# The first norm's gain spread by TensorE, the first product group ordered by hand, and a rewritten order of the attention stage

## The chip, the cores and the metric

The kernel runs on one core of a Trainium2 chip. The metric is device time in microseconds (us) of one execution; the median of three runs is given where runs are told of. A core has TensorE (PE in the profile; its weight loads are PEld), VectorE (DVE), ScalarE (ACT), GpSimd (POOL) and SyncE (SP, which here only issues DMAs).

## The reference

Two layers act on 256 tokens of width 1024, all in f32. A SwiGLU block (inner width 2816) stands at both ends of each layer. Between them layer 0 has a pooling mixer and layer 1 an attention mixer with 8 heads in each of 3 groups of different dilation. Every part has an RMS norm in front and one behind it, before the residual sum:

```python
def rms_norm(x, gain):
    y = x32 * lax.rsqrt(jnp.mean(x32 * x32, axis=-1, keepdims=True) + RMS_EPS) * gain

f = swiglu(rms_norm(h, g[0]), ffn_w_gate[layer, 0], ffn_w_up[layer, 0], ffn_w_down[layer, 0])
h = h + 0.5 * rms_norm(f, g[1])
```

In the attention each query row takes a softmax over the keys of all three groups together (the mix over groups by their sums comes to that), multiplies the values by it, and goes through an output projection.

## The kernel before, in words

Tokens stand in two row blocks of 128 (`h[0]`, `h[1]`). To keep f32 accuracy with single-pass matmuls, each operand is split into a high part (a cast to fp32r on ScalarE, L100) and a low part (the rest, on VectorE, L101), and three products are summed. A weight block of 128 x 2048 comes by DMA into one of three `raw` buffers; its two halves are split into "units", which lie in six `hl` and two `xy` buffers. An operand `aT` is the normalised row block, transposed by TensorE in eight 128-column pieces and split the same way.

Opening. x is loaded in halves, the first norm's gain is loaded by a DMA that writes the same row to 128 partitions (`load_gain`, L176), 64 small matmuls run on zeros (`WARM`, L82), and the factor of each row (a sum of squares on ScalarE, the power -0.5 on GpSimd) and the gain are multiplied into the rows on VectorE (`norm`, L267). Then follow the transposes (L216) and the first product group of the first SwiGLU block: 96 matmuls of 512 columns into four PSUM banks (`acc_b0`). Instructions inside `tc.manual_schedule` keep the order in which they are written, for the engines that it names; all others are placed by a planner.

Norms between blocks (`Bound`). `first` multiplies a block's output by its gain and factor, adds it to h, and writes the rows for the next block into a second buffer, with the row factor of the previous norm; `second` transposes; `third` finds the new factor, which later steps multiply in. All inverse roots are powers on GpSimd.

Attention. For each of four head pairs `pr` and both row blocks `i`: a query projection in two halves (`q_proj`, 24 matmuls of 384 columns), the rope (L700 to L704, VectorE), transposes of the queries (`q_turn`, L819) with copies by ScalarE (L821), scores (`scores`, tile sc), then masking and a running maximum on VectorE (L759), the factor nm from it (L761), the exponential on ScalarE (L763), a reciprocal on VectorE (L769) and the multiplication by it on GpSimd (`over_sums`, L770), transposes of the probabilities (`p_turn`, L783) with copies by ScalarE (L786), and the product with the values (`values`, tile ob). A loop over `pr` writes them in this order (conditions and loads left out):

```python
q_proj(pr, 0, 0, cur); over_sums(pr - 1, 0); q_turn(pr - 1, 1); p_turn(pr - 2, 1)
q_proj(pr, 0, 1, cur); scores(pr - 1, 1); values(pr - 2, 1); p_turn(pr - 1, 0)
q_proj(pr, 1, 0, cur); over_sums(pr - 1, 1); q_turn(pr, 0); values(pr - 1, 0)
q_proj(pr, 1, 1, cur); scores(pr, 0)
```

Behind the loop the last pair's steps are mixed with the output projection (`o_proj`, tile acc_o), with only TensorE's order by hand. Below, a half pair is the time from one score group to the next.

Of the kernel before, what the change touches and what calls it, by code (L numbers as in the profile page):

```python
# [11 lines left out]
F32 = mybir.dt.float32  # L12
# [18 lines left out]
WARM = 64  # L31
# [17 lines left out]
def trunk_kernel(ctx: ExitStack, tc: tile.TileContext, x, pos, gains, pscale, ws, wq, invf, amask, pmat, icnt, out):  # L49
# [31 lines left out]
    for _ in range(WARM):  # L81
        nc.tensor.matmul(warm[:, 0:P], zeros, zeros, start=True, stop=True)  # L82
# [39 lines left out]
    def load_q_units(pr, b):  # L122
        raw = rawp.tile([P, 2, 1024], F32, tag="raw", name=f"rawq{pr}{b}")
        nc.sync.dma_start(raw[:, :, :768], wq[pr * 2 + b])
        return [parts(raw, k, 768, pr % 2 == 0 and b == 0) for k in range(2)]
# [68 lines left out]
    def post(i, f, gain, half, name, done=None):  # L194
# [81 lines left out]
    def ffn(n, aT, sums, boundary, middle=None, late=None, q=None):  # L276
# [121 lines left out]
        units = first_units + (load_units(4) if first_units else load_units(8, True))  # L398
        first_units[:] = []
        gu = [acc_pair(f"b{n}{i}") for i in range(2)]  # L400
        if n == 0:
            for z in range(2):
                both([gu[0][z], gu[1][z]], units[z * 4 : z * 4 + 4])
# [63 lines left out]
    class Bound:  # L467
# [15 lines left out]
        def first(self, i, f):  # L483
            self.y = []

            def scaled(i, c):
                if not self.y:
                    self.y.append(sc4.tile([P, D], F32, tag="y", name=f"n_{self.n}{i}"))
                nc.vector.scalar_tensor_tensor(
                    self.y[0][:, c], h[i][:, c], self.old[:, i : i + 1], self.gpre[:, c], op0=ALU.mult, op1=ALU.mult  # L490
                )

            post(i, f, self.gpost, self.half, self.n, scaled)

        def second(self, i):
            transposed(i, self.y[0], self.aT, self.n, self.sums)
# [20 lines left out]
    gpre = load_gain(0, "pre")  # L517
    aT = new_aT("x")
    sums = Sums("x")
    with tc.manual_schedule(engines={mybir.EngineType.DVE, mybir.EngineType.Activation}):  # L520
        y = norm(0, gpre, "x", rstd_of(h_halves(0), "qx0", rx[:, 0:1]))
        raws = [load_raw(at=0)]
        first_units += [parts(raws[0], 0, xy=True)]
        nc.sync.dma_start(h[1], x[P:, :])
        transposed(0, y, aT, "x", sums)
        rstd_of(h_halves(1), "qx1", rx[:, 1:2])
        load_raw(at=1, raw=raws[0])
        first_units += [parts(raws[0], 1, xy=True)]
        y = norm(1, gpre, "x", rx[:, 1:2])
        raws.append(load_raw())  # L530
        first_units += [parts(raws[1], 0)]
        transposed(1, y, aT, "x", sums)
        first_units += [parts(raws[1], 1)]
    for i in range(2):
        sums.add(i)
# [202 lines left out]
    qT = [qx[g // 2][:, g % 2].rearrange("p (r s) -> p r s", r=4) for g in range(3)]  # L738
    am = qx[2][:, 0].bitcast(BF16).rearrange("p (i k) -> p i k", i=2)
    pTt = [t.rearrange("p (c t) -> p c t", c=4) for t in (qx[1][:, 1, 0:512], qx[1][:, 1, 512:1024], qx[2][:, 1])]  # L740
    nc.gpsimd.dma_start(am, amask.rearrange("i p k -> p i k"))
    npt = [0]
    probs = {}

    def scores(pr, i, pool=accp, tag="acc"):
# [3 lines left out]
        sc = [pool.tile([P, 512], F32, tag=tag, name=f"sc{i}_{pr}{e}") for e in range(2)]  # L749
        for o, g, keys in ((0, 0, slice(0, S)), (256, 1, t), (384, 2, t)):  # L750
            for e in range(2):
                a = slice(e * 64, e * 64 + 64)
                n = keys.stop - keys.start
                mm(sc[e][:, o : o + n], q[g][a, t], kT[g][a, pr, keys], True, True)
        probs[i, pr] = []
        for e in range(2):
            p = sc2.tile([P, 512], F32, tag="w2", name=f"p{i}_{pr}{e}")
            mx = st.tile([P, 1], F32, tag="mx", name=f"mx{i}_{pr}{e}")
            nc.vector.tensor_tensor_reduce(p, sc[e], am[:, i], 1.0, -3.0e38, op0=ALU.add, op1=ALU.max, accum_out=mx)  # L759
            nm = st.tile([P, 1], F32, tag="nm", name=f"nm{i}_{pr}{e}")  # L760
            nc.vector.tensor_scalar_mul(nm, mx, -0.125)  # L761
            den = st.tile([P, 1], F32, tag="den", name=f"den{i}_{pr}{e}")
            nc.scalar.activation(p, p, AF.Exp, bias=nm, scale=0.125, accum_out=den)  # L763
            probs[i, pr].append((p, den))

    def over_sums(pr, i):
        for e, (p, den) in enumerate(probs[i, pr]):
            rd = st.tile([P, 1], F32, tag="rd", name=f"rd{i}_{pr}{e}")
            nc.vector.reciprocal(rd, den)  # L769
            nc.gpsimd.tensor_scalar_mul(p, p, rd)  # L770
            probs[i, pr][e] = p

    oT = [None, None]

    pT = {}

    def p_turn(pr, i):

        pT[i, pr] = []
        for e in range(2):  # L780
            tp = tpp.tile([P, 4, P], F32, tag="tp", name=f"ptp{i}_{pr}{e}")
            for c in range(4):
                nc.tensor.transpose(tp[:, c], probs[i, pr][e][:, c * P : (c + 1) * P], ident)  # L783
            pT[i, pr].append(pTt[npt[0] % len(pTt)])
            npt[0] += 1
            nc.scalar.copy(pT[i, pr][e], tp)  # L786

    def values(pr, i):
# [4 lines left out]
        for c, (g, j) in enumerate(((0, 0), (0, 1), (1, i), (2, i))):  # L793
            for e in range(2):
                n = slice((2 * pr + e) * 64, (2 * pr + e) * 64 + 64)
                mm(ob[e * 64 : e * 64 + 64, 0:P], vt[g][:, j, n], pT[i, pr][e][:, c], c == 0, c == 3)
# [3 lines left out]
    acc_f = [None, None]  # L800

    def o_proj(i, chunks):
# [5 lines left out]
    def q_proj(pr, i, half, units):  # L808
# [4 lines left out]
        if half == 1:  # L813
# [197 lines left out]
```

## Time and profile before

| | before |
|---|---|
| median of 3 runs | 970.23 us (968.0 to 972.78) |
| profiled execution | 972.42 us |
| its span, first to last instruction | 970.7 us |
| TensorE busy | 946.7 us, 4560 matmuls |
| VectorE busy | 682.6 us |
| ScalarE busy | 536.3 us |
| GpSimd busy | 62.7 us |
| mean granted TensorE clock | 0.986 |

Busy time counts overlapping work of one engine once. The granted clock is 1 at the upper of TensorE's two levels (2.4 GHz) and 0.5 at the lower (1.2 GHz). A wait is time in which an engine stood idle until something released it.

### The profile page before, as it was taken

What the parts mean: (1) busy time and instruction counts of PE and PEld (TensorE: products, weight loads), DVE (VectorE), ACT (ScalarE), POOL (GpSimd) and SP (SyncE); (2) the same over time, 40 slices, a digit from 0 to 9 for tenths busy, and PEclk for the clock granted to TensorE, in tenths of its full rate; (3) what the DMA queues carried; (4) which work ended last, traced back from release to release, by engine and by line L of the source; (5) the groups of instructions that cost most, each with busy time, mean ns of one, the idle gap of its engine ahead of it and who ended that gap; (6) DMA issues with size and microseconds to landing.
All of it is one profiled execution on the core that took longest, in us unless ns stands there. A gap on an engine that the chain in (4) does not pass through costs nothing.

```text
span 970.7 us, 12064 instructions
## 1 busy us (share of the span) xinstructions
PE 946.7 (98%) x4560; PEld 784.5 (81%) x4560; DVE 682.6 (70%) x768; ACT 536.3 (55%) x672; POOL 62.7 (6%) x74
## 2 busy tenths in 40 slices
PE   7999999999999999999999999999988899999997
PEld 5888788888888888888888888888976688888886
DVE  5879874488878886458887964875465587888642
ACT  5665753366657565355756643644345576675531
POOL 0000000010100000000000000200033310000000
PEclk8999999999999999999999999999999799999999
DMA  7887775565568597536687865564334236968721
GB/s 248 294 254 223 242 278 182 209 211 179 194 211 261 186 298 260 188 131 244 156 300 225 295 218 181 186 208 144 128 102 148 87 119 186 335 141 296 245 87 44
DMA packets 55898, 197.16 MB, mean 203 GB/s; under 512 B 7392, under 2 KB 7392, under 8 KB 53792
## 3 DMA queue, kind: packets, MB, share of 16 engines
q1 hardware_dynamic: 53456, 179.35, 52.5%
q0 software_dynamic: 2384, 17.04, 9.3%
q8 instruction: 36, 0.59, 0.2%
q14 instruction: 22, 0.18, 0.1%
HBM read 178.54 MB, written 1.05 MB: 185 GB/s over the span
## 4 chain that ended last, share of the span: by engine, by line
PE 92%; DVE 3%; ACT 2%; issue 1%; DMA 1%; POOL 0%; SPq 0%; DVEq 0%; POOLq 0%; ACTq 0%
PE acc_d L130 24%; PE st L323 15%; PE g L130 13%; PE u L130 9%; PE acc_b L130 9%; PE kp L130 3%; PE vp L130 3%; PE qp L130 3%; PE acc_w L130 2%; PE acc_u L130 2%; PE htp L304 2%; PE ob L130 1%; DVE hl L101 1%; DMA raw<-in_ws 1%; PE acc_o L130 1%
## 5 line engine op out<-in xcount | busy, mean ns | idle before, releaser
L101 DVE TENSOR_TENSOR hl<-raw,hl 128x1024 fp32r<-128x1024 f32 x182 | 221.0, 1221 | 110.8 <-ACT hl L100 110.1
L100 ACT CAST hl<-raw 128x1024 fp32r<-128x1024 f32 x182 | 189.5, 1051 | 147.2 <-PE acc_d L130 99.0
L130 PE MATMUL acc_d<-hl,h 128*128 128x512 f32 x1056 | 243.2, 390 | 0.0
L130 PEld LDWEIGHTS acc_d<-hl,h 128*128 128x128 f32 x1056 | 197.3, 188 | 40.4
L108 DVE TENSOR_TENSOR hl_lo<-xy,hl_hi 128x2048 fp32r<-128x2048 f32 x40 | 91.6, 2290 | 48.3 <-ACT hl_hi L107 48.3
L108 DVE TENSOR_TENSOR hl_lo<-raw,hl_hi 128x2048 fp32r<-128x2048 f32 x48 | 109.7, 2285 | 13.9 <-ACT hl_hi L107 13.8
L107 ACT CAST hl_hi<-xy 128x2048 fp32r<-128x2048 f32 x40 | 76.5, 1912 | 57.1 <-PE u L130 28.2
L107 ACT CAST hl_hi<-raw 128x2048 fp32r<-128x2048 f32 x48 | 91.9, 1914 | 23.9 <-PE st L323 11.5
L130 PE MATMUL acc_b<-hl,aT_m 128*128 128x512 f32 x192 | 44.4, 390 | 0.0
L130 PE MATMUL g<-hl_hi,aT_m 128*128 128x512 f32 x128 | 41.9, 393 | 0.0
L130 PEld LDWEIGHTS acc_b<-hl,aT_m 128*128 128x128 f32 x192 | 35.9, 188 | 7.4
L323 PE MATMUL st<-hl_hi,S_m 128*128 128x512 f32 x128 | 41.9, 393 | 0.0
L306 ACT CAST h<-htp 128x512 fp32r<-128x512 f32 (+1 forms) x48 | 26.3, 549 | 28.1 <-PE htp L304 28.1
L130 PE MATMUL u<-hl_hi,aT_m 128*128 128x512 f32 x128 | 41.8, 393 | 0.0
L130 PE MATMUL qp<-hl,aT_f 128*128 128x384 f32 x192 | 39.3, 357 | 0.0
L130 PEld LDWEIGHTS qp<-hl,aT_f 128*128 128x128 f32 x192 | 35.2, 200 | 1.3 <-issue 0.8
L130 PE MATMUL kp<-hl,aT_hk 128*128 128x512 f32 x144 | 34.5, 394 | 0.0
L340 POOL DMA_DIRECT2D xy<-raw x16 | 14.0, 876 | 298.5 <-ACT h L306 85.3
L130 PE MATMUL vp<-hl,aT_hk 128*128 128x512 f32 x144 | 33.1, 390 | 0.0
L770 POOL TENSOR_SCALAR p<-p,rd 128x512 f32<-128x512 f32 x16 | 24.9, 1563 | 116.0 <-DVE rd L769 94.3
L307 DVE TENSOR_TENSOR h<-htp,h 128x512 fp32r<-128x512 f32 (+1 forms) x48 | 30.7, 640 | 2.2 <-ACT h L306 2.0
L130 PEld LDWEIGHTS vp<-hl,aT_hk 128*128 128x128 f32 x144 | 27.0, 188 | 5.6
(261 smaller groups left out, 1592.6 us busy)
## 6 DMA issues: line engine op xcount, KB each, us to landing
raw<-in_ws SPq DMA_DIRECT2D x278, 512.0 KB, 4.9
xy<-in_ws SPq DMA_DIRECT2D x32, 512.0 KB, 6.5
xy<-raw POOLq DMA_DIRECT2D x16, 1024.0 KB, 8.2
rawq<-in_wq SPq DMA_DIRECT2D x8, 768.0 KB, 4.7
gain_post<-in_gains SPq DMA_DIRECT2D x14, 256.0 KB, 7.0
gain_pre<-in_gains SPq DMA_DIRECT2D x12, 256.0 KB, 7.3
rawpm<-in_pmat SPq DMA_DIRECT2D x2, 512.0 KB, 4.4
out_dram<-h SPq DMA_DIRECT2D x4, 256.0 KB, 2.1
```

What stands on the lines that cost most here:

```text
L100: nc.scalar.copy(hl[:, 0, :n], raw[:, k, :n])
L101: last["dve"] = nc.vector.tensor_sub(hl[:, 1, :n], raw[:, k, :n], hl[:, 0, :n])
L107: nc.scalar.copy(hi, raw)
L108: last["dve"] = nc.vector.tensor_sub(lo, raw, hi)
L130: last["mm"] = nc.tensor.matmul(o, l, r, start=start, stop=stop)
L304: nc.tensor.transpose(tp[:, k], prod[c, i][:, k * P : (k + 1) * P], ident)
L306: nc.scalar.copy(d[:, 0], tp[:, :nt])
L307: nc.vector.tensor_sub(d[:, 1], tp[:, :nt], d[:, 0])
L323: nc.tensor.matmul(ps, a(z, k), u[v], start=start and k == 0 and n == 0, stop=k == 3 and n == 2, skip_group_check=not start,)
L340: nc.gpsimd.dma_start(dst, src, accum_op=ALU.add)
L770: nc.gpsimd.tensor_scalar_mul(p, p, rd)
```

## The change

Opening: the gain is loaded as one row, and two matmuls with a row of ones write it to all 128 partitions of two PSUM banks, from where VectorE reads it. 26 matmuls on zeros run first and three times four more (`FILL`) between the products. A new function `opening` writes the order of TensorE, VectorE, ScalarE and SP up to the end of the first product group; one of the sums of squares goes to VectorE. The first row block's products with the first units come before the second row block's norm.

```diff
-WARM = 64
+WARM = 26
+FILL = 4
+    keep_warm(WARM)
+    gfirst = gp.tile([P, D], F32, tag="pre", name="gain_first")
+    nc.sync.dma_start(gfirst[0:1], gains[0:1])
...
+        with tc.manual_schedule(
+            engines={
+                mybir.EngineType.PE,
+                mybir.EngineType.DVE,
+                mybir.EngineType.Activation,
+                mybir.EngineType.SP,
+            }
+        ):
+            raws.append(load_raw())
+            nc.sync.dma_start(h[1], x[P:, :])
+            raws.extend(load_raw() for _ in range(2))
+            for k in range(2):
+                mm(gb[k], ones[0:1, 0:P], gfirst[0:1, k * 512 : (k + 1) * 512], True, True)
+            rs = rstd_x(0)
+            y = rows(0, rs)
+            turn_x(0, 0, y)
+            parts_x(0, 0)
+            turn_x(0, 1, y)
+            unit(0)
+            parts_x(0, 1)
+            keep_warm(FILL)
+            products(0, 0)
+            unit(1)
+            keep_warm(FILL)
+            products(0, 1)
+            keep_warm(FILL)
+            rs = rstd_x(1)
+            unit(2)
+            y = rows(1, rs)
+            sums.add(0)
+            unit(3)
+            raws.append(load_raw())
+            products(0, 2)
+            turn_x(1, 0, y)
+            parts_x(1, 0)
+            turn_x(1, 1, y)
+            parts_x(1, 1)
+            products(0, 3)
+            unit(4)
+            for j in range(4):
+                products(1, j)
+            for j in range(5, 8):
+                unit(j)
+            for i in range(2):
+                for j in range(4, 8):
+                    products(i, j)
+        sums.add(1)
```

Here `rows` is the normalising, `turn_x` the transposes, `parts_x` the high and low parts of the transposed rows, `unit` the split of a half weight block, and `products(i, j)` six matmuls of row block i with unit j. `rstd_x` keeps the power on GpSimd, as it was.

Norms: the rows for the next block are written over the buffer of the block's own output.

```diff
             if done is not None:
-                done(i, c)
+                done(i, c, y)
+        return y
```

Attention: masking and the factor nm become one instruction, the multiplication by the reciprocal goes from GpSimd to VectorE, three query copies become two, and three buffers for transposed probabilities become two. The order of TensorE, VectorE and ScalarE is written out up to the last pair, and a function `between` holds what stands behind each projection:

```diff
+        nc.vector.tensor_tensor_reduce(
+            p, sc[pr, i][e], am[:, i], -0.125, 3.0e38, op0=ALU.add, op1=ALU.min, accum_out=nm
+        )
...
-            nc.gpsimd.tensor_scalar_mul(p, p, rd)
...
+        nc.vector.tensor_scalar_mul(p, p, rd)
...
+    def between(b, q, new, old):
...
+        z = high(b)
+        if b < 9:
+            next_raw(b + 1)
+        q_rope(*q)
+        if new is not None:
+            score_mm(*new)
+            for e in range(2):
+                masked(*new, e)
+        if old is not None:
+            p_turn(*old)
+        if new is not None:
+            exped(*new, 0)
+        if old is not None:
+            for e in range(2):
+                p_copy(*old, e)
+        if new is not None:
+            exped(*new, 1)
+        u = low(z)
+        if new is not None:
+            for e in range(2):
+                over_sum(*new, e)
+        return u
...
+            q_proj(pr, 0, 0, cur)
+            if pr > 0:
+                q_turn(pr - 1, 1)
+            if pr > 1:
+                value_mm(pr - 2, 1)
+            q_proj(pr, 0, 1, cur)
+            units += between(2 * pr + 2, (pr, 0), (pr - 1, 1) if pr > 0 else None, (pr - 1, 0) if pr > 0 else None)
+            q_proj(pr, 1, 0, cur)
+            q_turn(pr, 0)
+            if pr > 0:
+                value_mm(pr - 1, 0)
+            q_proj(pr, 1, 1, cur)
+            units += between(2 * pr + 3, (pr, 1), (pr, 0), (pr - 1, 1) if pr > 0 else None)
+        raw = load_raw()
+        first_units += [parts(raw, k, xy=True) for k in range(2)]
+        o_proj(0, 0, 1)
         q_turn(3, 1)
+        value_mm(2, 1)
+        raw = load_raw()
+        o_proj(0, 2)
+        score_mm(3, 1, gup, "gu")
+        masked(3, 1, 0)
+        masked(3, 1, 1)
         p_turn(3, 0)
+        exped(3, 1, 0)
+        p_copy(3, 0, 0)
+        p_copy(3, 0, 1)
+        exped(3, 1, 1)
+        over_sum(3, 1, 0)
+        over_sum(3, 1, 1)
+        first_units += [parts(raw, k) for k in range(2)]
+        o_proj(1, 0)
+        value_mm(3, 0)
+        o_proj(1, 1)
+        o_proj(0, 3)
         go.first(0, acc_f[0])
+        p_turn(3, 1)
+        p_copy(3, 1, 0)
+        p_copy(3, 1, 1)
+        o_proj(1, 2)
+        value_mm(3, 1)
+        o_proj(1, 3)
         go.second(0)
```

`high` and `low` are the casts and the low parts of one query weight block (from block 8 on, of the output projection's), `q_rope`, `score_mm`, `value_mm` and `p_copy` the parts of the functions told above. `first_units` are four units of the last SwiGLU block, which before were split behind the attention.

## Rows read from the trace of the kernel before

**Rows 1.** The page: busy time, share and count of each engine, and the chain of work that ended last, by engine.

```profile
PE 946.7 (98%) x4560; PEld 784.5 (81%) x4560; DVE 682.6 (70%) x768; ACT 536.3 (55%) x672; POOL 62.7 (6%) x74
...
PE 92%; DVE 3%; ACT 2%; issue 1%; DMA 1%; POOL 0%; SPq 0%; DVEq 0%; POOLq 0%; ACTq 0%
```
**Rows 2.** The view by stretches of time. Columns: from and to, length, then busy time and count on PE, PEld, DVE, ACT and POOL, the granted clock, the busy share of the DMA engines, GB/s.

```profile
60.00:660.00 600.00, 598.92 (x2780) 494.88 (x2778) 447.74 (x470) 338.93 (x394) 25.52 (x35) 1.00 0.68 222
703.56:756.09 52.53, 44.97 (x317) 39.58 (x316) 33.01 (x79) 29.02 (x65) 17.68 (x12) 0.90 0.33 116
756.09:783.71 27.62, 24.39 (x157) 19.32 (x156) 16.75 (x39) 15.66 (x34) 8.94 (x7) 0.88 0.27 87
```
**Rows 3.** The chain of waits in order of time, from 0 to 45 us: start, length, engine or transfer, tile, line, count.

```profile
2.59 8.40 DMA raw<-in_ws
...
19.61 19.56 PE acc_b L130 x85
39.17 2.72 PE g L130 x12
```
**Rows 4.** The timeline from 0 to 25 us: start, length, engine, line, operation, tiles, and in brackets the idle time before it and its releaser.

```profile
4.66 0.63 ACT L183 ACTIVATE jk_qx<-h 128x512 bf16<-128x512 f32 x1 [0.51 <-DMA h<-in_x]
...
7.03 0.75 DVE L267 SCALAR_TENSOR_TENSOR n_x<-h,r_x,gain_pre 128x512 f32<-128x512 f32 x1 [1.47 <-DMA gain_pre<-in_gains]
...
9.81 0.75 DVE L267 SCALAR_TENSOR_TENSOR n_x<-h,r_x,gain_pre 128x512 f32<-128x512 f32 x1 [2.02 <-DMA gain_pre<-in_gains]
```
**Rows 5.** Groups of instructions from 0 to 40 us, shapes kept apart: line, engine, operation, count, then busy us, mean ns of one, and the idle time before them.

```profile
L101 DVE TENSOR_TENSOR hl<-raw,hl 128x1024 fp32r<-128x1024 f32 x8 | 9.7, 1220 | 2.6 <-ACT hl L100 2.6
L100 ACT CAST hl<-raw 128x1024 fp32r<-128x1024 f32 x8 | 8.1, 1049 | 5.6 <-DMA raw<-in_ws 5.6
L82 PE MATMUL warm<-zeros 128*128 128x128 bf16 x64 | 5.6, 273 | 1.0 <-DVE zeros L79 1.0
```
**Rows 6.** Stretches of the opening, columns as in rows 2.

```profile
5.04:8.45 3.41, 2.16 (x32) 1.79 (x29) 0.91 (x2) 0.34 (x2) 0.55 (x1) 1.00 0.95 255
8.45:11.87 3.42, 0.70 (x5) 0.42 (x4) 0.75 (x1) 0.86 (x1) 0.00 (x0) 0.98 1.01 388
11.87:15.28 3.41, 2.69 (x5) 1.70 (x6) 2.51 (x4) 3.38 (x9) 0.55 (x1) 0.50 1.02 416
15.28:18.70 3.42, 3.24 (x11) 2.03 (x10) 3.33 (x4) 1.97 (x4) 0.00 (x0) 0.52 0.52 172
```
**Rows 7.** Who waited for whom, TensorE from 689 to 784 us: us in total, times, longest.

```profile
PE ob L130 <- ACT qT L786: 5.8, 3, 2.6
PE ptp L783 <- POOL p L770: 2.7, 3, 1.4
PE qtp L819 <- DVE ra_q L704: 1.2, 1, 1.2
```
**Rows 8.** Groups of instructions from 689 to 790 us, as in rows 5.

```profile
L770 POOL TENSOR_SCALAR p<-p,rd 128x512 f32<-128x512 f32 x16 | 24.9, 1563 | 116.0 <-DVE rd L769 94.3 <-ACT qT L786 14.6 <-PE qtp L819 7.1
...
L763 ACT ACTIVATE p<-p,nm 128x512 f32<-128x512 f32 x16 | 11.5, 722 | 24.4 <-DVE nm L761 24.2
L759 DVE CUSTOM_DVE_ANT_0 p<-sc,qT 128x512 f32<-128x512 f32 x16 | 10.9, 685 | 5.0 <-PE sc L130 5.0
...
L786 ACT COPY qT<-ptp 128x512 f32<-128x512 f32 x16 | 8.8, 592 | 4.1 <-PE ptp L783 4.1
L100 ACT CAST hl<-rawq 128x768 fp32r<-128x768 f32 x10 | 7.9, 850 | 0.0
...
L703 DVE TENSOR_TENSOR rb_q<-qp,stab 128x192 f32<-128x192 f32 x16 | 4.9, 347 | 0.0
...
L700 DVE TENSOR_TENSOR ra_q<-qp,ctab 128x384 f32<-128x384 f32 x8 | 4.4, 552 | 5.6 <-PE qp L130 5.5
...
L761 DVE TENSOR_SCALAR nm<-mx 128x1 f32<-128x1 f32 x16 | 2.4, 153 | 0.5
...
L798 DVE TENSOR_TENSOR oT<-ob,oT 128x128 fp32r<-128x128 f32 x8 | 2.3, 290 | 10.2 <-ACT oT L797 10.2
```
**Rows 9.** The chain of waits from 684 to 790 us, as in rows 3.

```profile
697.14 1.83 DVE hl L101 x2
...
716.48 1.08 PE sc L130 x12
717.55 2.28 PE qp L130 x12
...
723.12 1.08 PE sc L130 x12
724.20 1.03 PE ob L130 x16
725.23 1.02 PE ptp L783 x8
...
782.48 1.39 PE acc_o L130 x6
```
**Rows 10.** A stretch of the attention in which TensorE mostly stood still, and the one from 749.1 on, columns as in rows 2.

```profile
746.00:749.70 3.70, 0.55 (x3) 0.31 (x3) 2.46 (x10) 2.31 (x7) 0.00 (x0) 0.91 0.98 354
749.10:755.90 6.80, 6.19 (x28) 5.56 (x28) 3.08 (x6) 4.75 (x10) 3.10 (x2) 0.50 0.29 111
```
**Rows 11.** DMA issues from 684 to 760 us: count, KB each, median us from issue to landing.

```profile
rawq<-in_wq SPq DMA_DIRECT2D x3, 768.0 KB, 4.6
```

More of the change, by code (lines that the diff above doesn't have):

```diff
@@ L80, in trunk_kernel, with keep_warm @@
     warm = gup.tile([P, 512], F32, tag="gu", name="warm")
-    for _ in range(WARM):
-        nc.tensor.matmul(warm[:, 0:P], zeros, zeros, start=True, stop=True)
+    def keep_warm(n):
+        for _ in range(n):
+            nc.tensor.matmul(warm[:, 0:P], zeros, zeros, start=True, stop=True)
+    keep_warm(WARM)
+    gfirst = gp.tile([P, D], F32, tag="pre", name="gain_first")
+    nc.sync.dma_start(gfirst[0:1], gains[0:1])
     block_no = [0]
@@ L120, in load_form, with load_q_raw @@
         return form(load_raw())
-    def load_q_units(pr, b):
+    def load_q_raw(pr, b):
         raw = rawp.tile([P, 2, 1024], F32, tag="raw", name=f"rawq{pr}{b}")
         nc.sync.dma_start(raw[:, :, :768], wq[pr * 2 + b])
-        return [parts(raw, k, 768, pr % 2 == 0 and b == 0) for k in range(2)]
+        return raw
     waiting = []
@@ L396, in pair @@
                 up(c + 1, i, g[i])
-        units = first_units + (load_units(4) if first_units else load_units(8, True))
-        first_units[:] = []
-        gu = [acc_pair(f"b{n}{i}") for i in range(2)]
         if n == 0:
-            for z in range(2):
-                both([gu[0][z], gu[1][z]], units[z * 4 : z * 4 + 4])
+            gu = opening()
+        else:
+            units = first_units + (load_units(4) if first_units else load_units(8, True))
+            first_units[:] = []
+            gu = [acc_pair(f"b{n}{i}") for i in range(2)]
         for i in range(2):
@@ L782, in p_turn, with p_copy, value_mm @@
             for c in range(4):
[L783 to L788, printed above, removed]
+                nc.tensor.transpose(tp[:, c], probs[pr, i, e][0][:, c * P : (c + 1) * P], ident)
+            pT[pr, i, e] = tp
+    def p_copy(pr, i, e):
+        nc.scalar.copy(pTt[e], pT[pr, i, e])
+    def value_mm(pr, i):
         if oT[i] is None:
@@ L812, in q_proj, with q_rope @@
             proj_mm(qp[i][:, :384], aT, i, units, 384, only=q)
[L813 to L814 removed]
+    def q_rope(pr, i):
+        qr[pr, i] = rope(qp[i][:, :384], i, 6, f"q{pr}{i}")
     def q_turn(pr, i):
@@ new lines, in q_turn, with next_raw, high @@
+        t = slice(i * P, (i + 1) * P)
+        nc.scalar.copy(q01[:, :, pr, t], tp[:, :2])
+        nc.scalar.copy(qT[2][:, pr, t], tp[:, 2])
+    raws = []
+    def next_raw(b):
+        raws.append(load_q_raw(b // 2, b % 2) if b < 8 else load_raw())
+    def high(b):
+        z = []
+        for k in range(2):
+            pool, tag = (xyp, "xy") if b in (0, 4) else (hlp, "hl")
+            hl = pool.tile([P, 2, 1024], F32R, tag=tag, name="hl")
+            n = 768 if b < 8 else 1024
+            nc.scalar.copy(hl[:, 0, :n], raws[b][:, k, :n])
+            z.append((hl, b, k, n))
+        return z
@@ new lines, in trunk_kernel @@
+    with tc.manual_schedule(
+        engines={mybir.EngineType.PE, mybir.EngineType.DVE, mybir.EngineType.Activation}
+    ):
+        for b in range(3):
+            next_raw(b)
+        units = low(high(0)) + low(high(1))
+        for pr in range(4):
+            cur, units = units, []
+            q_proj(pr, 0, 0, cur)
[14 more added lines that the diff above has]
+        o_proj(0, 0, 1)
+        q_turn(3, 1)
+        value_mm(2, 1)
[4 more added lines that the diff above has]
+        masked(3, 1, 1)
+        p_turn(3, 0)
+        exped(3, 1, 0)
[9 more added lines that the diff above has]
+        o_proj(0, 3)
```

188 lines of the change are left out of this document (84 added, 104 removed).

## The prediction

> **What bounds the kernel now.** I read the page's busy shares and its chain first [rows 1]: TensorE is busy 98% of the span and carries 92% of the chain, so only time in which it stands still, or runs at the lower of its two clock levels, can be won. The view by stages says where that is [rows 2]: in the 600 us from 60 to 660 it idles 1.1 us; in the attention loop from 703.56 to 756.09 it is busy 44.97 of 52.53 at a mean clock of 0.90; in the tail from 756.09 to 783.71, 24.39 of 27.62 at 0.88. A mean of 0.90 means that a fifth of the stretch ran at half speed, and half of that fifth is lost: 52.53 x 0.20 / 2 = 5.3 us in the loop, 27.62 x 0.24 / 2 = 3.3 in the tail. With the idle time 12.9 us can be had in the loop and 6.5 in the tail. The third place is the opening: the first group's products run without a break only from 19.61 to 39.17 [rows 3]. In front of them VectorE's normalising of the first rows starts at 7.03 and 9.81, each time when a gain transfer lands, and the first weight block lands at 10.99 [rows 3, 4].
>
> **The opening.** The change drops both 256 KB gain transfers. One 4 KB row and two matmuls of 512 columns with a column of ones take their place. Eight transposes of 128 columns (also plain f32) hold TensorE 1.02 us at the upper level [rows 9], so 0.51 per 512 columns and 1.0 at the lower; I take 1.0 for each spreading matmul, since TensorE will have paused after 26 warming matmuls. Bounds are 0.51 and, should each column need as many passes again, 2.0. Started near 5, when the row can have landed behind x, they are over by 7.
>
> The page "FP8 and Floating Point Precision" of the Trainium skill says under its notes on TensorE numerics that true FP32 takes four passes through the array; by that each would be 1.7 us at 1.2 GHz (an estimate), the second half of the rows would start near 8.6 instead of 7.3, and the opening's sum would be about 1 us worse.
>
> The first square sum stays on ScalarE, the second goes to VectorE at 4.66 for 0.69 (the masked reduction's price, rows 8), so the factor is ready near 6.4 and the rows are normalised by 8.0 (two of 0.75, rows 4), where the second half before ran from 9.81 to 10.56. The first weight block moves ahead of 0.5 MB; at the 255 to 388 GB/s of those stretches [rows 6] that is 1.3 to 2.0 us, so it lands near 9.3 and its cast (1.05) ends at 10.35. From there VectorE sets the order: four low parts at 1.22, three subtractions for the transposed rows at 0.69, the sum and two rows of the second half at 0.16 + 1.50 [rows 4, 5, 8], 8.6 in all, plus some 0.9 of waiting for casts: done by 19.9. The 24 products of the first rows on the gate's columns fit beside that. Then 72 of the 96 products stand in an unbroken line at 0.227 (2.72 per 12, rows 3): 16.3, so the group ends near 36.2 instead of 39.17, a gain of 3.0. Bounds: 0, if late casts eat it, and 4.5, if the block lands at 7.5. I take 2.5, because of the clock: it fell after 8.45 to 11.87, where TensorE was busy 0.70 of 3.42, and was still low in 15.28 to 18.70, busy 3.24 [rows 6].
>
> The page "TensorE: Matmul & The Clock Gate" (section "What's actually happening") says that throttled is the default and activity releases it. That speaks against cutting 64 warming matmuls to 26 and 12 fillers; the trace agrees as far as the clock stayed low behind the idle stretch. By it the opening's products up to 18.7 would run at half speed and the group would end near 37.4, a gain of 1.8 instead of 2.5.
>
> Costs at nothing: the fillers (12 x 0.09, from 5.6 us for 64, rows 5) stand where TensorE waits for the next unit; the sums of row block 0, now inside the written order, take ScalarE 2 x 0.6 between two casts; SP's order holds the fourth block until the first is split (near 13.5), and it is wanted at 21. What is won here reaches the end, since TensorE hardly waits behind it [rows 2].
>
> **The loop.** Between two score groups TensorE has the same work as before. Where nothing waited, from 716.48 to 723.12, such a half pair took 6.64 us, without a value group; with one (1.03) it is 7.7 [rows 9]. Five full half pairs follow 703.56: 38.5 us, where 52.53 were spent. The waits that made the difference are the value products behind the copies of transposed probabilities (5.8), the transposes behind GpSimd's multiplication (2.7), and a query transpose behind the rope (1.2) [rows 7]; the clock fell behind them, for instance after 746.0 to 749.7, where TensorE was busy 0.55 of 3.70 [rows 10].
>
> Can the new order keep up? Time is counted from the end of a half pair's projection. VectorE, in its written order: rope 2 x 0.55 + 2 x 0.35, less overlap 1.6; two masked reductions 1.4 (done at 3.05; the factor nm at 0.15 each goes); two low parts at 0.92 [rows 9], done at 4.9; two reciprocals and two multiplications; 0.29 for the value subtraction [rows 8]. A 512-element f32 multiplication by a column is not in this trace on VectorE: between 0.15 (one element) and 0.69 (two-tensor operations of that size, on this engine), with GpSimd's 1.56 as the far end. I take 0.69, the nearest in size and engine: in all 6.8 of 7.7. ScalarE: first exponential from 2.35 to 3.2, two copies until 4.25, second exponential until 5.15, two query copies and one of the output until 6.0, then two casts at 0.85: 7.7 with room only because the casts can begin before the next half pair starts. TensorE reaches the value products at 1.08 (scores) + 0.9 (transposes) + 2.09 (projection) + 0.4 (query turn) = 4.5 [rows 9], just after the copies. The probabilities are normalised by 6.5 and wanted at 7.7 + 1.1. Nothing waits by more than some 0.2; only once, where the second half of pair 0's successor meets its low parts, 0.3. So the loop ends 38.5 + 0.3 + 0.2 = 39.0 after 703.56: 13.5 won. Bounds: 14.2 (no wait) and 9.0, where VectorE sets the pace with 1.56 per multiplication: 6.8 + 2 x 0.87 = 8.5 per half pair. A transposed-probability buffer falls away (three to two): a copy then waits for the value products of one half pair back, long done.
>
> **The tail.** Here the new order has a hole. The scores of the last pair go into the two banks that a query transpose and a value group used. The value group's subtraction stands on VectorE behind the last multiplication (6.9) and two low parts of the next stage's first units (2 x 1.22): 9.65 after the loop's end, while TensorE, with two output projection pieces, the turn, the value group and a third piece behind its scores and transposes, is there at 1.08 + 0.9 + 2.78 + 0.4 + 1.05 + 1.39 = 7.6. It waits 2.1. Behind it in TensorE's queue are the transposes, the output projection and all the rest. Two more low parts delay the output subtraction ahead of the last product of row block 0 (1.6), and row block 1's last subtraction stands behind the norm (1.2). The work is eight projection pieces of 1.39 [rows 9], three value groups of 1.05, two score groups, three transpose groups of 0.9, 0.4 and 0.9 for the turns: 20.4. With some 6 of waiting it makes 26, where 27.6 were spent. If the clock falls behind the first wait, 6.8 us at half speed are 3.4 more. Bounds 21 and 29.5; I take 26.9: 0.7 won.
>
> **Everything else.** Normalising in place frees one buffer at each norm and makes VectorE alternate h and n; TensorE is not waiting there [rows 2]: 0.
>
> **Sum.** 2.5 + 13.5 + 0.7 = 16.7. The profiled execution took 972.4 with a span of 970.7 (1.7 lie around it): 955.7 by it. The median of the runs shown is 2.2 lower: 953.5.
>
> **The rivals.**
> VectorE sets the loop's pace. For it: 6.8 of 7.7 is tight, and with 1024-wide low parts (two half pairs) it is 7.4; against it: the multiplication would have to cost as on GpSimd. 8.5 per half pair: 4.5 less won, 958.
> The clock. For it: every idle stretch of some 2 us in this trace was followed by the lower level [rows 6, 10], and there are fewer warming matmuls and a 2.1 wait in the tail; against it: the loop has no such stretch. Opening at 0 instead of 2.5, tail at -2.7 instead of 0.7: 5.9 less won, 959.4.
> It doesn't do what it says: the copies stay behind the exponentials on ScalarE and the value products wait for them as now; half pairs of 10.2 remain, the loop wins 1.5 and the rest 2: within 0.5%.
> Slower: each half pair's ScalarE order begins with the casts of a query block, and if that has not landed, exponentials, copies and query turns wait behind them, TensorE behind those. The block is issued one half pair ahead; landing took 4.6 us [rows 11], 3.1 less than the 7.7. Five half pairs must grow by 16.7 / 5 = 3.3 before the gain is gone: landing above 11.0 us. At 12 it would be 975. Against it: the DMA engines are a third busy in the loop [rows 2].
>
> **Chances and range.** Forecast 0.70, VectorE 0.10, clock 0.09, not doing it 0.05, slower 0.06. The forecast's own span: opening 0 to 4.5, loop 12 to 14.2, tail -1.5 to 6: 946 to 960. The range takes that and the two near rivals: 946.5 to 961. A measurement of this kernel can tell about 0.5%, 4.9 us, from no change; faster by more than that: 0.70 + 0.10 + 0.09 = 0.89; within it 0.05; slower 0.06.
>
> **What would show it.** The first group's last product near 36.7, with the rows normalised by 8.0; score groups 7.7 apart and no TensorE wait over 0.5 in the loop; an upper clock through it; multiplications on VectorE at 0.69 or less; a wait of about 2 in front of the last pair's scores; gate products of the last block some 27 after the loop's end. It is wrong if half pairs stay above 9, or if the stages behind the opening or the attention give time back.

## The result and the profile after

The changed kernel takes 956.89 us (median of 4 runs, 955.95 to 957.32) against 970.06 before (4 runs): a ratio of 0.986, interval 0.984 to 0.989, so 13.2 us faster. 953.5 was forecast. The profiled execution took 956.8 with a span of 955.0, 15.7 less than the span before. One execution of the kernel e1_pool_mul below took 1744.38 us at a mean granted clock of 0.795, a slow state that no other execution here shows, and it is left out of that kernel's numbers.

The page, its busy times and chain by engine, after [rows 1]:

```profile
PE 942.8 (99%) x4538; PEld 778.4 (82%) x4538; DVE 686.9 (72%) x770; ACT 533.8 (56%) x662; POOL 36.5 (4%) x59
...
PE 94%; DVE 3%; issue 1%; ACT 1%; DMA 0%; SPq 0%; DVEq 0%; POOLq 0%; POOL 0%; ACTq 0%
```

TensorE's matmuls are the same but for the opening (38 small ones on zeros instead of 64, and the spreading of the gain). Of the 15.7 us its busy time gave 3.9 (946.7 to 942.8); the other 11.8 were idle time. The chain of waits of the changed kernel says where (start, length, engine, tile, line, count):

```profile
4.13 3.74 PE gain_x L137 x4
7.87 1.06 PE tp_x L565 x4
...
8.96 0.59 ACT aT_x L570
9.54 0.95 ACT hl L107
...
10.54 2.27 PE acc_b L137 x6
...
17.58 17.75 PE acc_b L137 x78
35.33 2.72 PE g L137 x12
...
699.87 1.08 PE sc L137 x12
...
707.69 1.08 PE sc L137 x12
...
766.53 8.57 PE acc_b L137 x30
...
790.95 2.72 PE g L137 x12
```

The first group ends at 35.33 instead of 39.17 [rows 3]: 3.8 won. Two score groups lie 707.69 - 699.87 = 7.82 apart; over five half pairs TensorE is busy all of the 39.20 us (first row below). The stages after, columns as in rows 2:

```profile
699.87:739.07 39.20, 39.20 (x317) 35.27 (x317) 30.51 (x75) 24.12 (x55) 0.00 (x0) 1.00 0.39 131
739.07:766.50 27.43, 23.98 (x155) 17.85 (x155) 23.04 (x43) 18.53 (x39) 1.29 (x3) 0.93 0.51 179
...
762.00:765.00 3.00, 1.52 (x5) 1.23 (x6) 1.67 (x5) 1.35 (x5) 0.74 (x2) 0.64 0.20 79
765.00:767.00 2.00, 1.88 (x8) 1.47 (x7) 1.67 (x2) 2.00 (x5) 0.00 (x0) 0.50 0.00 0
767.00:770.00 3.00, 3.00 (x9) 2.28 (x9) 2.94 (x7) 1.79 (x5) 0.55 (x1) 0.56 0.57 186
```

The loop, the first row, is full and at the upper clock: 39.2 against 52.53, 13.3 won. The tail is not better. Up to the first gate product it takes 27.5 (766.53 - 738.98), against 27.6 before. It goes on at the lower clock into the gate products (30 in 8.57, against 6.8 at the upper level), so I measure it up to the group behind them: from the start of the loop's last score group by the timeline (756.09 before, 738.98 after) to the first product on g in the chain. All tails below are counted so. It was 50.5 before and is 52.0 after: 1.5 lost. 3.8 + 13.3 - 1.5 = 15.6, nearly the whole 15.7 by which the spans differ: between these two executions nothing more than 0.2 is won or lost elsewhere. TensorE's waits from 685 to 776 (us in total, times, longest) are all in the tail:

```profile
PE acc_o L137 <- DVE oT L896: 2.4, 2, 2.1
PE sc L137 <- DVE oT L896: 0.5, 1, 0.5
PE acc_o L137 <- ACT oT L895: 0.4, 1, 0.4
```

The 5.8, 2.7 and 1.2 of rows 7 are gone. The timeline of the tail, on VectorE and in its last line on TensorE, names the longest wait (start, length, engine, line, operation, tiles):

```profile
759.15 0.74 DVE L213 SCALAR_TENSOR_TENSOR h<-y_m,rs_pm,h 128x512 f32<-128x512 f32 x1
...
759.88 1.22 DVE L108 TENSOR_TENSOR hl<-raw,hl 128x1024 fp32r<-128x1024 f32 x1
...
761.03 0.74 DVE L493 SCALAR_TENSOR_TENSOR y_m<-h,r_f,gain_pre 128x512 f32<-128x512 f32 x1
761.69 0.74 DVE L213 SCALAR_TENSOR_TENSOR h<-y_m,rs_pm,h 128x512 f32<-128x512 f32 x1
762.47 0.75 DVE L493 SCALAR_TENSOR_TENSOR y_m<-h,r_f,gain_pre 128x512 f32<-128x512 f32 x1
...
763.14 0.28 DVE L896 TENSOR_TENSOR oT<-ob,oT 128x128 fp32r<-128x128 f32 x1
...
763.48 1.22 PE L137 MATMUL acc_o<-hl,oT 128*128 128x512 f32 x2 [2.13 <-DVE oT L896]
```

The value subtraction that TensorE wants stands behind row block 0's whole norm on VectorE, and inside that norm stands a low part of the next stage's weights (759.88).

### The profile page after: what moved, and what is told of

It reads as the page before. It is cut to its first block, busy times and chain, and to the rows that moved or that the text cites. A ratio compares the mean times of both kernels' runs of the same rounds, so it can differ in the third digit from the quotient of the medians.

```text
span 955.0 us, 11976 instructions
## 1 busy us (share of the span) xinstructions
PE 942.8 (99%) x4538; PEld 778.4 (82%) x4538; DVE 686.9 (72%) x770; ACT 533.8 (56%) x662; POOL 36.5 (4%) x59
## 4 chain that ended last, share of the span: by engine, by line
PE 94%; DVE 3%; issue 1%; ACT 1%; DMA 0%; SPq 0%; DVEq 0%; POOLq 0%; POOL 0%; ACTq 0%
PE acc_d L137 24%; PE st L331 16%; PE g L137 13%; PE acc_b L137 9%; PE u L137 9%; PE qp L137 4%; PE kp L137 3%; PE vp L137 3%; PE acc_w L137 2%; PE acc_u L137 2%; PE htp L312 2%; PE sc L137 1%; DVE hl L108 1%; PE ptp L880 1%; PE yp L137 1%
## 5 line engine op out<-in xcount | busy, mean ns | idle before, releaser
L108 DVE TENSOR_TENSOR hl<-raw,hl 128x1024 fp32r<-128x1024 f32 x178 | 215.9, 1221 | 106.6 <-ACT hl L107 105.8
L107 ACT CAST hl<-raw 128x1024 fp32r<-128x1024 f32 x178 | 185.2, 1051 | 140.0 <-PE acc_d L137 99.4
L114 ACT CAST hl_hi<-raw 128x2048 fp32r<-128x2048 f32 x48 | 91.8, 1913 | 20.5 <-PE st L331 11.3
L137 PE MATMUL qp<-hl,aT_f 128*128 128x384 f32 x192 | 37.2, 342 | 0.0
L137 PEld LDWEIGHTS qp<-hl,aT_f 128*128 128x128 f32 x192 | 32.9, 188 | 1.3 <-issue 0.9
L331 PE MATMUL st<-hl_hi,aT_m 128*128 128x512 f32 x96 | 31.0, 391 | 0.0
L137 PEld LDWEIGHTS kp<-hl,aT_hk 128*128 128x128 f32 x144 | 26.6, 188 | 5.4
```

Of the source, the lines that this page charges most:

```text
L107: nc.scalar.copy(hl[:, 0, :n], raw[:, k, :n])
L108: last["dve"] = nc.vector.tensor_sub(hl[:, 1, :n], raw[:, k, :n], hl[:, 0, :n])
L114: nc.scalar.copy(hi, raw)
L137: last["mm"] = nc.tensor.matmul(o, l, r, start=start, stop=stop)
L331: nc.tensor.matmul(ps, a(z, k), u[v], start=start and k == 0 and n == 0, stop=k == 3 and n == 2, skip_group_check=not start,)
```

## The experiments

Ratios are to the kernel before on the same chip, with their 95% interval.

**One part each.** Theory: the loop is the gain (over 10), the opening gives 2 to 4, the multiplication's move is only part of the loop's gain. Rivals: the move to VectorE is the whole loop gain, or the opening's gain is lost behind it.

e1_pool_mul puts the multiplication back on GpSimd in the changed kernel.

```diff
-        nc.vector.tensor_scalar_mul(p, p, rd)
+        nc.gpsimd.tensor_scalar_mul(p, p, rd)
```

> The changed kernel with one edit: the multiplication by the reciprocal sum goes back to GpSimd, in the same written order. Theory (the written order made the gain): in the loop the probabilities are wanted 8.8 us after a half pair's projection and two multiplications of 1.56 on GpSimd, the first started near 5.2, end by 8.3, so half pairs stay at 7.8 and the time stays within 1 us of the changed kernel's 957, in the tail perhaps 1 us more. Rival (moving the multiplication to VectorE made the gain): transposes of probabilities wait as before, by 0.5 to 1.4 each, half pairs grow to 8.5 or more and the time to 961 or more.

957.09 us (957.03 to 957.75, three executions), ratio 0.986 (0.983 to 0.989): as the changed kernel. e1b_pool_mul is the same kernel, with the trace that is read here.

> A second look at the multiplication on GpSimd in the new order, for its trace. Theory (the written order made the gain): half pairs of 7.8 to 7.9, no wait of TensorE on GpSimd in the loop, multiplications near 1.56. Rival (the move made it): transposes wait for GpSimd, half pairs above 8.3.

957.41 in its one execution. One of TensorE's waits in that trace is on GpSimd (others left out):

```profile
PE ptp L880 <- POOL p L873: 0.4, 1, 0.4
```

One half pair took 8.5, the others 7.84 on the mean, and the tail 50.6. At GpSimd's 1.56 [rows 8] the multiplication still comes in time in all half pairs but one: in the new order its move is worth 0.6 in this trace, less than the totals can tell.

e2_old_order_dve does the reverse, the move alone in the kernel before.

```diff
-            nc.gpsimd.tensor_scalar_mul(p, p, rd)
+            nc.vector.tensor_scalar_mul(p, p, rd)
```

> The kernel before with one edit: the multiplication by the reciprocal sum on VectorE, where it takes 0.49 instead of 1.56, in the old order. Theory (the written order made the gain): only the waits behind GpSimd, 2.7 us, and part of the low clock behind them can go, while the value products still wait behind ScalarE's copies: 965 to 969. Rival (the move made the gain): most of the loop's 13 us come, 957 to 960.

966.46, ratio 0.996 (0.994 to 0.9975): some 4 us. Its waits of TensorE behind ScalarE and the rope, from 685 to 776:

```profile
PE ob L130 <- ACT qT L786: 5.7, 3, 2.5
PE qtp L819 <- DVE ra_q L704: 1.2, 1, 1.2
```

The wait on GpSimd is gone, the two others of rows 7 stand as they were, and the loop takes 50.6 instead of 52.5 (52.0 in e3_open_only, which has the old loop too). So some 1.9 of the loop's 13.3 come with the move alone, and the rest needs the new order or what was rewritten with it: the mask and factor in one instruction and the changed numbers of buffers, which no run takes out by themselves.

The tail is another matter. Before, TensorE waited twice there for GpSimd:

```profile
763.58 0.66 PE L783 MATMUL ptp<-ident,p 128*128 128x128 f32 x4 [1.36 <-POOL p L770]
...
765.12 0.66 PE L783 MATMUL ptp<-ident,p 128*128 128x128 f32 x4 [0.89 <-POOL p L770]
```

From 766.2 to 773.0 the granted clock then read 0.51. In e2_old_order_dve both waits are gone and the clock reads 1.00 up to the gate products. Its chain (the score group starts at 756.86 by the timeline):

```profile
756.93 0.88 PE sc L130 x8
...
803.82 2.72 PE g L130 x12
```

That is a tail of 47.0, 3.5 less than before, in the old order and by this one edit. The profiled execution was the slowest of ten (969.97): between the first group and the loop it lost 3.6, 2.0 of it in one wait of transposes (tp_kv) that the traces of before and after do not have.

e3_open_only takes the new opening alone, e4_attn_only all but the opening (the same lines the other way round).

```diff
-            for z in range(2):
-                both([gu[0][z], gu[1][z]], units[z * 4 : z * 4 + 4])
+            gu = opening()
...
-    gpre = load_gain(0, "pre")
```

> The kernel before with the new opening alone (old norms, old attention). Theory: the opening's 3.8 us, read at the start of the second product group, reach the end whole: 966.2 against 970. Rival (later stages are held by the weight stream or VectorE and give it back): 969 to 970, with the gain gone by the start of the attention.

967.67, ratio 0.996 (0.9945 to 0.998): between the theory's 966.2 and the rival's 969. The first group ends at 35.41, and from there to the loop the trace takes 664.2, where before took 664.4: the gain is not given back. Its span is 4.5 shorter than that of rows 2's execution, which was itself 2.4 above its median.

> The kernel before with all of the change but the opening. Theory: loop 13.3 won, tail and the group behind it 1.4 lost, so 11.9 less than before: 958 to 961, and together with the opening alone it adds up to the whole change. Rival (the parts depend on each other, as by the clock's state or the buffers): the two gains miss the whole by more than 2 us.

960.97, ratio 0.990 (0.987 to 0.993): half pairs of 7.84, the first group ends at 38.28, the tail takes 50.7. By the ratios the parts are worth 3.7 and 9.8, the whole 13.5 (by the medians 2.7 and 9.4, the whole 13.2): they add up within their intervals. 9.4 to 9.8 is 2 less than the theory's 11.9; the trace loses 2.2 between the first group and the loop, 2.0 of it in the same wait as e2's.

**Warming and fillers.** f3_nofill leaves the fillers out, f4_nowarm 25 of the 26 warming matmuls as well.

```diff
-WARM = 26
-FILL = 4
+WARM = 1
+FILL = 0
```

> The changed kernel without the three times four filling matmuls of the opening. Theory (the wide gain matmuls, the transposes and the early products keep TensorE busy enough by themselves, and VectorE sets the opening): the clock rises at the same place and the time is within 0.5 us of the changed kernel's 957. Rival (the fillers raise the clock): it rises one step later, and the opening ends 1 to 3 us later, 958 to 960.

> The changed kernel with 1 warming matmul instead of 26 and no fillers. Theory (the gain matmuls and what follows raise the clock, warming does not matter): within 0.7 us of 957. Rival (the first 3 us of warming matter): the clock rises later, near 15 to 19, the products run at half speed up to there and the opening ends 1 to 3 us later: 958 to 960.

958.99 (0.986, 0.983 to 0.988) and 957.04 (0.985, 0.983 to 0.987). 958.99 lies outside the first theory's range and in its rival's, 957.04 in the second theory's. The openings speak against both rivals, which had them end 1 to 3 us later. The first group ended at 35.95 and 35.77; with warming and fillers it ended at 35.33 after the change, and between 34.27 and 35.49 in all eight traces of this opening. Of TensorE in f4_nowarm the timeline shows:

```profile
0.98 0.29 PE L85 MATMUL warm<-zeros 128*128 128x128 bf16 x1 [0.98 <-DVE zeros L80]
3.85 3.75 PE L137 MATMUL gain_x<-gain_first,ones 1*128 1x512 f32 x4 [2.58 <-DMA gain_first<-in_gains]
```

It stood still for 2.6 us, and the gain matmuls took what they took behind 26 warming ones (3.74). Against 35.33, leaving out the fillers costs 0.6 and leaving out both 0.4 in the traces, less than the totals can tell. f3's trace also loses 3 us between 251 and 436 behind a late transfer, in stages that its edit does not touch; that the edit did not bring this on is likely and not shown.

**The tail.** Theory: the wait of 2.1 is the value subtraction behind the norm, and the clock's fall follows from it. Rivals: the norm's own chain sets the time, or the planner's placing of the next units. f1_tail splits the norm's step, puts the last turn and the last subtraction ahead of the part that writes h and the next rows, and the last piece of row block 0 behind them. f2_fill gives TensorE 30 matmuls of zeros in front of the last output piece.

```diff
-        o_proj(0, 3)
-        go.first(0, acc_f[0])
         p_turn(3, 1)
...
+        o_proj(0, 3)
+        go.first(0, acc_f[0], False)
...
+        go.first(0, None)
```

```diff
+        for _ in range(30):
+            nc.tensor.matmul(fill[:, 0:P], zeros, zeros, start=True, stop=True)
```

> The changed kernel with a new order in the tail: the last probabilities are turned and copied ahead of row block 0's last output product, and row block 1's last value subtraction stands on VectorE ahead of the two steps that update h and write the next rows. Theory (the wait of 2.1 us on that subtraction and the low clock behind it cost the tail its gain): the wait falls below 0.6, the gate products of the last block start 3 to 3.5 us earlier and run at the upper level, the second group begins 4 to 5 us earlier: 952 to 953.5. Rival (row block 0's norm itself sets the start of the next block, whatever stands beside it): the wait only moves to the transposes of that norm, 956 to 957.

> The changed kernel with 30 small matmuls on zeros in front of row block 1's last output product, where TensorE waits for 2.1 us. Theory (half of the tail's loss is the clock that falls behind that wait): the wait for the subtraction ends at the same moment, but the transposes and the first 30 gate products run at the upper level, 1.9 to 0.9 and 8.6 to 6.8: 2.5 us less, 954.5. Rival (what the clock costs there is hidden behind row block 1's norm): 956.5 to 957.5.

956.01 (0.984, 0.981 to 0.987; 953.18 to 958.3) and 955.80 (0.9835, 0.981 to 0.986): both fell short of the theory, and neither is clear of f4_nowarm's 957.04 (956.43 to 958.42), which ran beside them with the tail unchanged. f1_tail's trace is from its fastest execution. The waits of TensorE in its tail (one of 0.5 in front of the scores, as after the change, left out):

```profile
PE acc_o L137 <- ACT oT L905: 0.9, 1, 0.9
PE tp_m L231 <- DVE y_m L500: 0.8, 1, 0.8
PE acc_b L137 <- ACT aT_m L233: 0.8, 1, 0.8
PE acc_o L137 <- DVE oT L906: 0.8, 1, 0.8
```

The one wait of 2.1 became four of 0.8 to 0.9; casts and low parts of the last units still lay around and between the norm's steps on ScalarE and VectorE. The tail took 49.3. In f2_fill the clock stayed up, where after the change it read 0.64 and 0.50 (columns as in rows 2):

```profile
763.00:767.00 4.00, 2.48 (x14) 1.90 (x14) 2.67 (x7) 3.18 (x9) 0.74 (x2) 1.00 0.00 0
```

That the filling matmuls kept it up is not shown, since it also stayed up in f4_nowarm, which has none there. The norm's steps ran as before and TensorE waited 1.2 for its transposed rows: tail 50.7. That points to the second rival, the norm stretched by other work, which f5_tail_units tests.

r_after is the changed kernel once more, as the partner of f5_tail_units on one chip. f5 is f1 with the last block's units written in explicitly, two behind the turned probabilities and two behind the transposed rows of row block 0.

```diff
-            units = first_units + (load_units(4) if first_units else load_units(8, True))
+            units = list(first_units) if first_units else load_units(8, True)
...
+        raw = load_raw()
+        first_units.append(parts(raw, 0))
...
+        first_units.append(parts(raw, 1))
```

> The changed kernel again, unedited, beside the next three on one chip: 956 to 958, as the reference for them.

> The new tail order of the run before, and the last four units of the last block's first group also in written places: two behind the turned probabilities, two behind row block 0's transposes, where the planner had put their casts and low parts between the steps of row block 0's norm. Theory (in the tail the norm's chain of ScalarE and VectorE steps, stretched by other work placed inside it, sets the start of the next block): without them the gate products start 1.5 to 2 us earlier than in the run before and the second group begins 4 to 5 us earlier, counted from the loop's end, than in the changed kernel: 952 to 954. Rival (the norm's own latency is what is left): no change against the run before, 955 to 956.5.

956.18 (0.984, 0.9815 to 0.987; 955.56 to 959.09) and 952.68 (0.980, 0.978 to 0.983; 952.29 to 953.77), as the theory had it: the tail takes 47.4 against r_after's 50.8, and the gate products start 23.9 us behind the loop's last score group instead of f1_tail's 25.7.

**How much of the order has to be written?** e5_pe_only keeps TensorE's written order and leaves VectorE and ScalarE to the planner, in loop and tail.

```diff
-        engines={mybir.EngineType.PE, mybir.EngineType.DVE, mybir.EngineType.Activation}
+        engines={mybir.EngineType.PE}
```

> The changed kernel with only TensorE's attention order by hand, VectorE and ScalarE left to the planner. Theory (the order across the three engines made the loop's gain): waits of TensorE of 0.5 or more come back in the loop, half pairs of 8.3 to 9.5 on the mean, 959 to 966. Rival (TensorE's order alone, with value products a half pair later, made it): half pairs stay within 0.1 of 7.83 and the time within 1 us of the changed kernel.

951.92 (951.04 to 952.96), ratio 0.979 (0.976 to 0.982): the theory fell, and this is the fastest median, below all six executions of r_after; f5_tail_units overlaps with it. Its chain of waits:

```profile
700.73 1.08 PE sc L137 x12
...
708.58 1.08 PE sc L137 x12
...
739.94 1.08 PE sc L137 x12
...
764.81 6.18 PE acc_b L137 x26
...
786.83 2.72 PE g L137 x12
```

Half pairs of (739.94 - 700.73) / 5 = 7.84, as with the whole order written, and a tail of 47.0 (its last score group starts at 739.87), as long as e2's. VectorE's timeline in the tail:

```profile
757.69 1.41 DVE L213 SCALAR_TENSOR_TENSOR h<-y_m,rs_pm,h 128x512 f32<-128x512 f32 x2
759.02 1.41 DVE L493 SCALAR_TENSOR_TENSOR y_m<-h,r_f,gain_pre 128x512 f32<-128x512 f32 x2
760.34 0.28 DVE L896 TENSOR_TENSOR oT<-ob,oT 128x128 fp32r<-128x128 f32 x1
```

The norm's steps stand in one piece, and the subtraction behind them comes 20.5 us behind the loop's last score group instead of 24.2 (763.14 - 738.98) in the changed kernel.

## Why the prediction was right, and where it was off

**Opening: 2.5 forecast, 3.8 measured between the two profiles.** An unbroken line of products sets the end, as forecast, and the group ended at 35.33 where 36.7 was forecast. Of the 3.8, 0.9 belongs to the profiled execution of before, whose first group ended at 39.17 where the same opening in e2 and e4 ended at 38.25 and 38.28; the change itself is worth 2.9. That this is near the 3.0 of the sum before its discount is partly luck, for three of the sum's steps were off.

The first is the path to the first products. The first block's cast ended at 10.5 (10.35 forecast), but not because the block landed near 9.3: it had landed near 7.9. The cast stood on ScalarE behind the one for the transposed rows (8.96), and that behind the transposes and the gain matmuls. The term of the spreading matmuls was too small there: 1.0 each was taken, 3.74 / 2 = 1.87 measured, near the bound of 2.0, and the second half of the rows came at 7.91 instead of 7.3. The Trainium skill's page "FP8 and Floating Point Precision" (section "TensorE Precision Notes") says four passes, from which 1.7 was estimated; the measured 1.87 is nearer to that than to 1.0. In three other traces of this opening, e3_open_only, f1_tail and f5_tail_units, the two took 1.95 to 2.23 together, so 1.0 to 1.1 each. Whether the longer ones cost anything at the end is open: the first products then began at 9.3 to 9.9 instead of 10.54, and the group ended at 35.41, 34.27 and 35.49.

The second is the unbroken line: it began at 17.58 with 78 products, not at 19.9 with 72. The third is the discount for the clock: the first six products, from 10.54, took 2.27 (0.38 each, against 0.227 at the upper level), but behind them TensorE had work with hardly a break, and in f4_nowarm the group ended only 0.4 later. The prediction had the group end at 37.4 by the rule that the throttled state is the default ("TensorE: Matmul & The Clock Gate", section "What's actually happening", of the Trainium skill). It ended at 35.3: the rule itself fits the durations of the first matmuls (last section), but the lower level did not last up to 18.7.

**Loop: 13.5 forecast, 13.3 measured (39.0 and 39.2 us).** No engine but TensorE sets the pace, as forecast: VectorE is busy 30.5 of 39.2 and ScalarE 24.1. The prediction's first paragraph put only 12.9 within reach, less than it then forecast. Its 5.3 for the clock was too low, as the mean of 0.90 counts idle time too: for the same 317 matmuls TensorE's busy time fell from 44.97 to 39.20, by 5.8. The multiplication was oversized; by form, from 685 to 776:

```profile
L873 DVE TENSOR_SCALAR p<-p,rd 128x512 f32<-128x512 f32 x16 | 7.8, 487 | 0.6
```

0.487, not 0.69, so VectorE had more room than I gave it. The rival "VectorE sets the pace" did not come, and e1 shows that it would not have come at GpSimd's price either.

What the gain comes from I had half right. Most of it is not the multiplication's engine: 1.9 by e2, and 0.6 by e1b in the new order. Nor does it need the new written order on VectorE and ScalarE (e5): TensorE's new order with the planner for the rest does as well. What is left is TensorE's new order, the end of the old written order on VectorE and ScalarE, the mask and factor in one instruction, and the changed buffers; no run parts these. The two traces show one thing that stood in the way; VectorE's timeline of before, behind the score group at 703.56:

```profile
704.24 2.26 DVE L101 TENSOR_TENSOR hl<-rawq,hl 128x768 fp32r<-128x768 f32 x2 [1.05 <-ACT hl L100]
706.43 0.55 DVE L700 TENSOR_TENSOR ra_q<-qp,ctab 128x384 f32<-128x384 f32 x1
```

and after, behind the one at 699.87:

```profile
699.91 0.56 DVE L795 TENSOR_TENSOR ra_q<-qp,ctab 128x384 f32<-128x384 f32 x1 [0.21 <-PE qp L137]
...
702.72 1.82 DVE L939 TENSOR_TENSOR hl<-rawq,hl 128x768 fp32r<-128x768 f32 x2
```

Before, two low parts of the next query block ran ahead of the rope, which began 2.9 us after the projection's end; now it begins at once and the low parts come behind the masking. That these low parts alone make the old half pairs long is read from the traces and not tested: the kernel before with the planner on VectorE and ScalarE, and its own order on TensorE, was not run.

**Tail: 0.7 won forecast, 1.5 lost.** This is the step that failed, inside its bounds. Up to the first gate product, as it was forecast, the tail took 27.5 where 26.9 was forecast and 27.6 was spent before, so 0.1 won; the loss comes with the gate products. That 27.5 is near 26.9 is luck, as the terms show. The wait in front of the last pair's scores was 0.5 instead of 2.1. The two low parts stood in front of the value subtraction as forecast:

```profile
745.37 2.35 DVE L108 TENSOR_TENSOR hl<-raw,hl 128x1024 fp32r<-128x1024 f32 x2
747.64 0.28 DVE L896 TENSOR_TENSOR oT<-ob,oT 128x128 fp32r<-128x128 f32 x1
```

But the subtraction was over 8.9 us after the loop's end instead of 9.65, and TensorE began the scores at 7.8 (7.6 forecast) and ran two of their twelve matmuls before it waited. The wait of the last subtraction, 1.2 in the forecast, became 2.1, since a low part of the next stage stood inside the norm of row block 0 (759.88); I had priced the norm as an unbroken piece. And the work was priced too low: 20.4 forecast, where f4_nowarm, with the same tail and the upper level all through, keeps TensorE busy 22.8 of its 27.2. The waits were priced too high to match: the three named ones add up to 4.9, the sum took some 6, and f4_nowarm's tail has 4.5.

Then the clock fell, as I had said could follow a first wait, but later and into the gate products. The fall is not sure. Here are 8 us by the view of stretches (columns as in rows 2), in r_after, which is the same kernel, and in f4_nowarm, whose tail is written the same (it starts 1.4 later there; moved by that, its row still reads 1.00):

```profile
762.00:770.00 8.00, 6.25 (x24) 4.94 (x25) 6.57 (x13) 5.28 (x12) 1.28 (x3) 0.79 0.31 105
```

```profile
762.00:770.00 8.00, 4.56 (x22) 3.05 (x21) 6.64 (x13) 5.06 (x13) 0.97 (x3) 1.00 0.31 101
```

After the change, the same 8 us read 0.57. The tails took 50.8 and 50.6, against 52.0 after and 50.5 before. So in the execution of after the fall is worth some 1.3, all but 0.2 of what the tail lost; without it the new tail is as long as the old one. What it could have won was there: splitting the norm's step brings it to 49.3 in one trace (f1_tail), the units' places to 47.4 (f5_tail_units), the planner's order to 47.0 (e5_pe_only). The step from f1_tail to f5_tail_units moves only the next block's units out of the norm, so the norm broken up by that work kept the tail long.

What I overlooked is e2's 47.0: in the old order the move of the multiplication alone makes the tail as short as the best of these. The old tail was long by the waits on GpSimd and the lower clock behind them; the change took these away and put the broken-up norm in their place. By e5_pe_only, the written order of VectorE and ScalarE cost the tail some 3.6 (50.6 against 47.0).

**Rivals and sum.** No half pair waited for a query block, and the waits on the copies are gone, so "slower" and "not doing it" found nothing. 2.5 + 13.5 + 0.7 = 16.7 against 15.6 measured between the profiles: the tail's 2.2 and the loop's 0.2 too much, less the opening's 1.3 too little. Most of the 3.4 by which the median missed is another thing: the profiled execution of before was 2.4 above its median, and I carried that over as if the next one would be too; it took 956.8, its median.

## What to carry to other kernels

When an engine that does not bound the kernel has an order written by hand, look at what that order puts ahead of the chain which the bounding engine waits for; try first to write only the bounding engine's order and leave the others to the planner (951.9 here, against 956.2 with all three written). Keep casts and low parts for later stages out from between the steps of a norm, by the planner or by explicit places. Read what each single edit does to every stage, not only to the one it was meant for: here one moved instruction had already shortened the tail by 3.5, and the rewrite around it gave that back. And put the first profile's distance from its median into the range, not into the forecast.

## What the runs showed that I had not expected

The granted clock's column reads 1.00 in the first microseconds, but the durations say otherwise: the 26 warming matmuls of the changed kernel take 2.95 us, 0.113 each, the fillers behind 12.8 us take 0.24 for four, 0.06 each. So in this execution TensorE was at the lower level until its first products ran, and only the durations tell that.

The same multiplication of 512 f32 elements by one factor per row takes 0.487 on VectorE and 1.56 on GpSimd, and two-tensor operations of that size take 0.69 on VectorE. And the same wait of 2.1 us in the same written tail was followed by the lower clock in four traces (after, r_after, f3_nofill, e1b_pool_mul) and not in two (e4_attn_only, f4_nowarm): one profile of a stretch cannot tell whether a fall belongs to the kernel.
